# Decay rows of a Mamba-2 scan: stored head by head, and broadcast from ScalarE's DMA queue instead of GpSimd's

## The chip, the core and the metric

One core of one Trainium2 chip runs the whole kernel. The metric is the device time of one execution in microseconds (us). Before the change it is 2491.99 us, the median of three runs (2491.88, 2491.99 and 2496.45). About 0.2%, some 5 us, is the smallest change that such a measurement can tell from none.

## The reference, cut to what matters

One encoder layer on 512 tokens of width 2048: an adaLN-modulated RMSNorm, one input projection, an HGRN2 mixer (8 heads) and a Mamba-2 SSD mixer (4 groups of 4 heads), an output projection, then a gated convolutional FFN and a last norm. The change touches one factor of the SSD mixer, the decay matrix `seg`:

```python
acum = jnp.cumsum((dt * a_head).transpose(0, 1, 3, 4, 2), axis=-1)
seg = jnp.exp(jnp.where(mask, acum[..., :, None] - acum[..., None, :], -jnp.inf))
cb = jnp.einsum('bctgn,bcsgn->bcgts', cm, bm)
y_diag = jnp.einsum('bcgts,bcgrts,bcsgrp->bctgrp', cb, seg, xdt)
```

For each of the 16 heads the kernel needs acum(t) along the free axis, the same in all 128 partitions, minus acum(s) per partition.

## The kernel before, in words

All large products run on TensorE as three matmuls (L168 to L170, the product of a rounded high part and a low part). A weight chunk of 256 rows by 512 columns is loaded by SyncE into a buffer `raw` (L148), rounded by ScalarE to `whi` (L163), and VectorE takes the rest as `wlo` (L164). There are five `raw` buffers and two each of `whi` and `wlo`. The modulation vectors come from a second stream of loads: `m` from `w_mod` (L184), 512 KB each, uses the same five buffers and the same SyncE queue, and VectorE folds each into `macc` with one instruction per half (L191).

While a projection streams through, small pieces of the mixers are put between its matmuls. Here these are `ssd_mix(g)` for groups 0, 3, 2, 1, two at a time, between 287 and 456 us of the span. Its steps, in the order of the text:

- `cbm` (L425, L429): four matmuls of C and B, masked by VectorE.
- `decay(h)` for each of four heads (L433 to L443): one row of `acrow` in DRAM is broadcast to all partitions of a tile `mm` (L436), then VectorE adds the per-partition term (L439) and clamps (L441), ScalarE takes the exponential (L442), VectorE multiplies by `cbm` (L443). `mm` is one of nine buffers of 128 x 512 that all small temporaries share.
- transposes (L451, L464), states (L474 to L482), and per head the product of `mm` with `xdt` (L489), whose result VectorE adds to `y` (L494); for three heads also the contribution of the state (L499, L501, L505).

The small products use only two PSUM banks (`mis`), so a small matmul can wait until VectorE has read an earlier one; TensorE takes its instructions in order, and then the projection behind it waits too.

`acrow` is made once by `ssd_dt` (L398 to L401): 64 rows, one per quarter of the sequence and head, of 128 tokens, stored by a DMA of GpSimd's queue at 260 us.

The order on each engine is fixed when the program is built, by the tile scheduler. Every engine issues in order: a DMA issue that waits for a buffer holds back what stands behind it on that engine. DMAs of the hardware queues (SyncE's and ScalarE's) also take turns on eight completion semaphores, shown below as DMAHW0 to DMAHW7, and a DMA is issued only when the one before it on its semaphore has landed. GpSimd's DMAs have semaphores of their own (DMASW).

Of the kernel before, what the change touches and what calls it, by code (L numbers as in the profile page):

```python
# [7 lines left out]
F32 = mybir.dt.float32  # L8
# [6 lines left out]
P = 128  # L15
S = 512
# [18 lines left out]
def hybrid_block_kernel(  # L35
# [6 lines left out]
    nc = tc.nc  # L42
# [22 lines left out]
    def T(name="t", dtype=F32):  # L65
        return tmp.tile([P, 512], dtype, tag="t", name=nm(name))
# [10 lines left out]
    def MIS(name="mis"):  # L77
        return psm.tile([P, 512], F32, tag="mis", name=nm(name))
# [4 lines left out]
    def CT(shape, name, dtype=F32):  # L83
        return cst.tile(shape, dtype, tag=name, name=name)
# [3 lines left out]
    def bc(ap, shape):  # L88
        return ap.unsqueeze(len(ap.shape)).broadcast_to(shape)
# [265 lines left out]
        A.activation(out=xbc[g][:, which, :], in_=y, func=AF.Silu)  # L355

    drm = ctx.enter_context(tc.tile_pool(name="drm", bufs=1, space=bass.MemoryType.DRAM))
    acrow = drm.tile([64, P], F32, tag="acrow", name="acrow")
    dtt = CT([P, 64], "dtt")
    dta = CT([P, 64], "dta")  # L360
    negb = CT([P, 16, 4, 2], "negb")
# [2 lines left out]
    def ssd_dt(src):  # L364
        pt = MIS()
        for t in range(NT):
            PE.transpose(out=pt[:, t * P:(t + 1) * P], in_=src[:, t * P:(t + 1) * P], identity=ident)
        xb, e, z, z2, p = (T(s_)[:, 0:64] for s_ in ("xb", "en", "zz", "z2", "pp"))

        def c4(t_):  # L370
            return t_.rearrange("p (c h) -> p c h", c=4)

        V.tensor_tensor(out=c4(xb), in0=c4(pt)[:, :, 0:16], in1=dtb.unsqueeze(1).broadcast_to([P, 4, 16]), op=ALU.add)
        V.tensor_tensor(out=c4(xb), in0=c4(pt)[:, :, 64:80], in1=c4(xb), op=ALU.add)
        V.scalar_tensor_tensor(out=e, in0=xb, scalar=-1.0, in1=xb, op0=ALU.mult, op1=ALU.min)
        A.activation(out=e, in_=e, func=AF.Exp)
        V.tensor_scalar(out=z, in0=e, scalar1=2.0, scalar2=None, op0=ALU.add)
        V.reciprocal(out=z, in_=z)
        V.tensor_tensor(out=z, in0=z, in1=e, op=ALU.mult)
        V.tensor_tensor(out=z2, in0=z, in1=z, op=ALU.mult)  # L380
        V.tensor_scalar(out=p, in0=z2, scalar1=1.0 / 19, scalar2=None, op0=ALU.mult)
        for k in (17, 15, 13, 11, 9, 7, 5, 3):
            V.scalar_tensor_tensor(out=p, in0=p, scalar=1.0 / k, in1=z2, op0=ALU.add, op1=ALU.mult)
        V.scalar_tensor_tensor(out=p, in0=p, scalar=1.0, in1=z, op0=ALU.add, op1=ALU.mult)
        V.tensor_scalar(out=xb, in0=xb, scalar1=0.0, scalar2=None, op0=ALU.max)
        V.scalar_tensor_tensor(out=dtt, in0=p, scalar=2.0, in1=xb, op0=ALU.mult, op1=ALU.add)
        V.tensor_tensor(out=c4(dta), in0=c4(dtt), in1=an.unsqueeze(1).broadcast_to([P, 4, 16]), op=ALU.mult)
        pc = MIS()
        for i, m in enumerate((tri, suf, ones, tri64, l1m)):
            PE.matmul(out=pc[:, i * 64:(i + 1) * 64], lhsT=m, rhs=dta, start=True, stop=True)  # L390
        A.activation(out=e3.rearrange("p a b -> p (a b)"), in_=pc[:, 0:192], func=AF.Exp)
        V.tensor_scalar(out=negb[:, :, :, 0].rearrange("p h c -> p c h"),
                        in0=pc[:, 192:256].rearrange("p (c h) -> p c h", h=16),
                        scalar1=-1.0, scalar2=None, op0=ALU.mult)
        V.tensor_copy(out=negb[:, :, :, 1].rearrange("p h c -> p c h"),
                      in_=pc[:, 256:320].rearrange("p (c h) -> p c h", h=16))
        pr = MIS()
        PE.matmul(out=pr[0:64, 0:P], lhsT=dta, rhs=tri64, start=True, stop=True)  # L398
        ar = T("acr")
        V.tensor_copy(out=ar[0:64, 0:P], in_=pr[0:64, 0:P])  # L400
        nc.gpsimd.dma_start(out=acrow, in_=ar[0:64, 0:P])  # L401

    def ssd_mix(g):

# [28 lines left out]
        def decay(h):  # L433
            hh = 4 * g + h
            m = mt[h] = T("mm")
            nc.gpsimd.dma_start(out=m.rearrange("p (c t) -> p c t", c=4),  # L436
                                in_=acrow.rearrange("(c h) t -> h c t", h=16)[hh].partition_broadcast(P))
            m8 = m.rearrange("p (a t) -> p a t", a=8)
            V.tensor_tensor(out=m8, in0=m8, in1=bc(negb[:, hh, :, :].rearrange("p c b -> p (c b)"), [P, 8, 64]),  # L439
                            op=ALU.add)  # L440
            V.tensor_scalar(out=m, in0=m, scalar1=0.0, scalar2=None, op0=ALU.min)  # L441
            A.activation(out=m, in_=m, func=AF.Exp)  # L442
            V.tensor_tensor(out=m, in0=m, in1=cbm, op=ALU.mult)  # L443

        decay(0)
        for cp in range(2):
            ps = MIS()
            for cc in range(2):
                for b in range(2):
                    t = 2 * cp + cc  # L450
# [33 lines left out]
        for h in range(4):  # L484
            if h < 3:
                decay(h + 1)
            ps = MIS()
            for cch in range(4):
                PE.matmul(out=ps[:, cch * HD:(cch + 1) * HD], lhsT=mt[h][:, cch * P:(cch + 1) * P],  # L489
                          rhs=xdt[:, cch, h * HD:(h + 1) * HD], start=True, stop=True)  # L490
                yield 0
            for cp in range(2):
                yh = ycols(cp)[:, :, h * HD:(h + 1) * HD]
                V.tensor_tensor(out=yh, in0=yh, in1=ps[:, cp * 128:(cp + 1) * 128].rearrange("p (t f) -> p t f", t=2),  # L494
                                op=ALU.add)
            if h < 3:
                ps = MIS()
                cch = h + 1
                PE.matmul(out=ps[:, 0:256], lhsT=xb[:, 3, cch * P:(cch + 1) * P], rhs=hst[h], start=True, stop=True)  # L499
                t = T("yo")[:, 0:256]  # L500
                V.tensor_tensor(out=t.rearrange("p (h f) -> p h f", h=4),  # L501
                                in0=ps[:, 0:256].rearrange("p (h f) -> p h f", h=4),
                                in1=bc(eac[:, cch, hs], [P, 4, HD]), op=ALU.mult)
                yo = yv(cch)[:, g * 256:(g + 1) * 256]
                V.tensor_tensor(out=yo, in0=yo, in1=t, op=ALU.add)  # L505
                yield 0
# [255 lines left out]
    for st, k0, k1 in SEGMENTS:  # L762
# [44 lines left out]
        if k1 == KT and st == 2:  # L807
            ssd_dt(dtraw)
# [54 lines left out]
    for j in range(2):  # L863
# [5 lines left out]
        for t in range(NT):  # L869
            sg = T("gs")  # L870
            A.activation(out=sg, in_=accs[t], func=AF.Silu)
            for i in range(4):
                h = 4 * j + i
# [208 lines left out]
```

## Time and profile before

| What | Value |
|---|---|
| median of three runs | 2491.99 us |
| profiled execution, own time | 2497.32 us |
| its span, first to last instruction | 2495.6 us |
| TensorE busy | 2416.4 us, 97% |
| VectorE busy | 1490.2 us, 60% |
| ScalarE busy | 783.7 us, 31% |
| GpSimd busy | 55.7 us, 2% |
| data moved by DMA | 335.86 MB, mean 135 GB/s |
| the 16 broadcasts `mm<-acrow` | 256 KB each, 9.2 us from issue to landing (median) |

Times in the profile are microseconds from the start of the span. A wait is named by the engine and line that waited, an arrow, and the line that ended it. "acc" tiles are projection accumulators, "mis" tiles the small PSUM banks. The column PEclk is the clock that TensorE was granted, 1.00 being the full one.

### The profile page before, as it was taken

How to read it: one execution, taken by the hardware profiler on the slowest of the kernel's cores; microseconds unless marked ns; L12 is line 12 of the kernel's file. 1: busy time of each engine (PE TensorE's matmuls, PEld its weight loads, DVE VectorE, ACT ScalarE, POOL GpSimd, SP SyncE). 2: the span in 40 equal slices, each digit the busy share in tenths (PEclk: the TensorE clock that was granted, in tenths of full speed). 3: DMA queues.
4: the chain of work that ended last, by engine and by line, in shares of the span. 5: the costliest groups of instructions: out<-in, count | busy, mean ns of one | idle time of the engine just before them, and what ended most of it. 6: DMA issues, size and time to landing. Idle time of an engine off the chain costs nothing.

```text
span 2495.6 us, 28998 instructions
## 1 busy us (share of the span) xinstructions
PE 2416.4 (97%) x11071; PEld 1987.7 (80%) x11071; DVE 1490.2 (60%) x2262; ACT 783.7 (31%) x1135; POOL 55.7 (2%) x80
## 2 busy tenths in 40 slices
PE   6999998999999999999999999999999999999998
PEld 5777877788777777887888888888888888888887
DVE  6884866666776656668536363636354545454557
ACT  6323422333332322433232222222222222222323
POOL 4000000000000000000000000000000000000000
PEclk9999999999999999999999999999999999999999
DMA  9883575344555656366333323233333333332332
GB/s 289 257 273 105 116 128 107 90 118 135 168 161 187 243 189 199 121 220 219 93 101 93 101 93 100 94 98 96 96 99 95 100 94 101 93 101 93 102 127 85
DMA packets 262823, 335.86 MB, mean 135 GB/s; under 512 B 18092, under 2 KB 182524, under 8 KB 261404
## 3 DMA queue, kind: packets, MB, share of 16 engines
q1 hardware_dynamic: 260432, 327.42, 41.8%
q0 software_dynamic: 1568, 4.31, 2.3%
q10 hardware_dynamic: 684, 2.28, 0.3%
q8 instruction: 87, 1.43, 0.2%
q14 instruction: 52, 0.43, 0.1%
HBM read 329.72 MB, written 4.23 MB: 134 GB/s over the span
## 4 chain that ended last, share of the span: by engine, by line
PE 76%; DMA 11%; DVE 9%; issue 2%; ACT 2%; POOL 0%; SPq 0%; DVEq 0%; ACTq 0%; POOLq 0%
PE acc L170 24%; PE acc L168 24%; PE acc L169 24%; DMA m<-in_w_mod_dram 8%; DVE wlo L164 3%; DVE macc L191 2%; DMA raw<-in_w_in_dram 1%; DVE macc L240 1%; DMA x<-in_x_dram 1%; ACT whi L163 1%; PE mis L570 1%; POOL rstd L267 0%; DMA mm<-acrow 0%; PE mis L612 0%; DVE att L577 0%
## 5 line engine op out<-in xcount | busy, mean ns | idle before, releaser
L164 DVE TENSOR_TENSOR wlo<-raw,whi 128x1024 fp32r<-128x1024 f32 (+1 forms) x408 | 490.3, 1203 | 707.7 <-ACT whi L163 703.2
L163 ACT CAST whi<-raw 128x1024 fp32r<-128x1024 f32 (+2 forms) x416 | 424.6, 1022 | 1304.4 <-PE acc L169 512.2
L168 PE MATMUL acc<-hhi,whi 128*128 128x512 f32 x1920 | 770.1, 402 | 10.7 <-ACT whi L163 6.1
L170 PE MATMUL acc<-hhi,wlo 128*128 128x512 f32 x1920 | 750.1, 393 | 3.1 <-DVE wlo L164 3.1
L169 PE MATMUL acc<-hlo,whi 128*128 128x512 f32 x1920 | 751.7, 392 | 0.0
L168 PEld LDWEIGHTS acc<-hhi,whi 128*128 128x128 f32 x1920 | 362.2, 189 | 88.2 <-ACT whi L163 10.2
L170 PEld LDWEIGHTS acc<-hhi,wlo 128*128 128x128 f32 x1920 | 362.3, 189 | 83.0 <-DVE wlo L164 6.1
L169 PEld LDWEIGHTS acc<-hlo,whi 128*128 128x128 f32 x1920 | 362.8, 189 | 69.5 <-issue 1.2
L191 DVE SCALAR_TENSOR_TENSOR macc<-m,cT,macc 128x512 f32<-128x512 f32 x240 | 180.0, 750 | 127.9 <-DMA m<-in_w_mod_dram 124.5
L168 PE MATMUL acc<-whi,act 128*128 128x512 f32 x640 | 249.0, 389 | 0.0
L169 PE MATMUL acc<-wlo,act 128*128 128x512 f32 x640 | 249.0, 389 | 0.0
L170 PE MATMUL acc<-whi,act 128*128 128x512 f32 x640 | 249.0, 389 | 0.0
L168 PE MATMUL acc<-whi,hhi 128*128 128x512 f32 x384 | 163.2, 425 | 0.0
L170 PE MATMUL acc<-whi,hlo 128*128 128x512 f32 x384 | 153.7, 401 | 0.0
L169 PE MATMUL acc<-wlo,hhi 128*128 128x512 f32 x384 | 152.8, 398 | 0.0
L170 PEld LDWEIGHTS acc<-whi,act 128*128 128x128 f32 x640 | 120.1, 188 | 25.0
L168 PEld LDWEIGHTS acc<-whi,act 128*128 128x128 f32 x640 | 120.1, 188 | 24.9
L169 PEld LDWEIGHTS acc<-wlo,act 128*128 128x128 f32 x640 | 120.1, 188 | 24.9
L994 DVE TENSOR_TENSOR g<-acc,gate 128x512 f32<-128x512 f32 x160 | 105.4, 685 | 3.8
L995 DVE TENSOR_TENSOR x<-x,g 128x512 f32<-128x512 f32 x160 | 105.3, 684 | 0.0
L168 PE MATMUL acc<-mhi,whi 128*128 128x512 f32 x256 | 105.2, 411 | 0.0
L170 PE MATMUL acc<-mhi,wlo 128*128 128x512 f32 x256 | 101.1, 395 | 2.3 <-DVE wlo L164 2.3
(274 smaller groups left out, 2193.9 us busy)
## 6 DMA issues: line engine op xcount, KB each, us to landing
raw<-in_ffn_w_up_dram SPq DMA_DIRECT2D x352, 256.0 KB, 2.9
m<-in_w_mod_dram SPq DMA_DIRECT2D x128, 512.0 KB, 4.1
raw<-in_ffn_w_down_dram SPq DMA_DIRECT2D x88, 512.0 KB, 3.6
m<-in_w_mod_dram SPq DMA_DIRECT2D x128, 256.0 KB, 4.2
raw<-in_w_in_dram SPq DMA_DIRECT2D x96, 256.0 KB, 3.9
raw<-in_w_in_dram SPq DMA_DIRECT2D x48, 512.0 KB, 4.0
raw<-in_w_out_dram SPq DMA_DIRECT2D x32, 512.0 KB, 4.5
x<-in_x_dram SPq DMA_DIRECT2D x8, 1024.0 KB, 10.8
```

The lines of the kernel that those rows point to most:

```text
L163: A.copy(out=h_, in_=r_)
L164: V.tensor_tensor(out=l_, in0=r_, in1=h_.bitcast(F32), op=ALU.subtract)
L168: PE.matmul(out=ps, lhsT=lh, rhs=rh, start=first, stop=False)
L169: PE.matmul(out=ps, lhsT=lh, rhs=rl, start=False, stop=False)
L170: PE.matmul(out=ps, lhsT=ll, rhs=rh, start=False, stop=last)
L191: V.scalar_tensor_tensor(out=acc, in0=last[:, k, :], scalar=cT[:, kt:kt + 1], in1=acc, op0=ALU.mult, op1=ALU.add)
L240: V.scalar_tensor_tensor(out=acc, in0=m[:, k, :], scalar=cT[:, kt:kt + 1], in1=acc, op0=ALU.mult, op1=ALU.add)
L570: PE.matmul(out=o, lhsT=kk[:, pr * P:(pr + 1) * P], rhs=halves(q, lv, True, base=pr * P, pairs=1), start=True, stop=True)
L994: V.tensor_tensor(out=m, in0=accs[t], in1=gates[5][:, cs], op=ALU.mult)
L995: V.tensor_tensor(out=x1[t][:, cs], in0=x1[t][:, cs], in1=m, op=ALU.add)
```

## The change

`acrow` is laid out with one row of 512 tokens per head instead of 64 rows of 128. The store (L401) scatters its 64 rows accordingly and stays on GpSimd's queue. Each broadcast (L436) then reads one contiguous row of 2 KB per partition instead of four pieces of 512 B, and it is issued by ScalarE on its hardware queue instead of by GpSimd on the software queue. From L437 on, the lines of the changed file are one lower than before.

```diff
-    acrow = drm.tile([64, P], F32, tag="acrow", name="acrow")
+    acrow = drm.tile([16, S], F32, tag="acrow", name="acrow")
...
-        nc.gpsimd.dma_start(out=acrow, in_=ar[0:64, 0:P])
+        nc.gpsimd.dma_start(out=acrow.rearrange("h (c t) -> c h t", c=4), in_=ar[0:64, 0:P])
...
             m = mt[h] = T("mm")
-            nc.gpsimd.dma_start(out=m.rearrange("p (c t) -> p c t", c=4),
-                                in_=acrow.rearrange("(c h) t -> h c t", h=16)[hh].partition_broadcast(P))
+            nc.scalar.dma_start(out=m, in_=acrow[hh].partition_broadcast(P))
```

The 16 broadcasts leave GpSimd's stream, where nothing stood between them, and now stand among ScalarE's roundings and exponentials. SyncE's order is the same as before; TensorE's and VectorE's differ in places by one to four instructions between 310 and 456 us of the old span.

The first place is ScalarE around 307 us: the convolution of the last group (`cy`, `xbc`), roundings (`whi`), and the first exponentials of `mm`. Before:

```order
L351 ACTIVATE cy_2446<-xbc_128,p_679 128x512
L163 CAST whi_2649<-raw_2648 128x1024
L355 ACTIVATE xbc_128<-cy_2446 128x512
L442 ACT_TABLE_LOAD
L442 ACTIVATE mm_2511<-mm_2511 128x512
L442 ACTIVATE mm_2524<-mm_2524 128x512
```

After:

```order
L351 ACTIVATE cy_2446<-xbc_128,p_679 128x512
L436 DMA mm_2511<-acrow 128x512
L436 DMA mm_2524<-acrow 128x512
L436 DMA mm_2710<-acrow 128x512
L163 CAST whi_2649<-raw_2648 128x1024
L436 DMA mm_2723<-acrow 128x512
L355 ACTIVATE xbc_128<-cy_2446 128x512
L441 ACT_TABLE_LOAD
L441 ACTIVATE mm_2511<-mm_2511 128x512
L441 ACTIVATE mm_2524<-mm_2524 128x512
```

The first four broadcasts, which GpSimd issued from 286.70 us on, now come behind the last convolution step of ScalarE.

The second place is ScalarE around 376 us, where the second pair of groups begins; these rows are of the changed program, with the semaphores that each waits for:

```order
L163 CAST whi_3090<-raw_3089 128x1024 [waits DMAHW0_49,DMAHW1_49,DVE_49,PE_49]
L436 DMA mm_3048<-acrow 128x512 [waits DMAHW5_49]
L436 DMA mm_3061<-acrow 128x512 [waits DMAHW7_49]
L436 DMA mm_3259<-acrow 128x512 [waits DMAHW1_49]
L436 DMA mm_3272<-acrow 128x512 [waits DMAHW3_49]
L441 ACTIVATE mm_3048<-mm_3048 128x512 [waits DVE_49]
L441 ACTIVATE mm_3061<-mm_3061 128x512 [waits DVE_49]
L163 CAST whi_3137<-raw_3136 128x1024 [waits DMAHW2_49,PE_49,Activation_49]
```

In the program before, the rounding `whi_3137` stood ahead of the exponential of `mm_3061`, and the four broadcasts were issued by GpSimd between 356 and 362 us. The wait on DMAHW3 at the last of them is for the load `m_3236` of the modulation stream, that on DMAHW1 for a piece of `raw_3229`.

The third place is ScalarE around 434 us, at the last two heads of the second pair. Before:

```order
L163 CAST whi_3509<-raw_3508 128x1024
L442 ACTIVATE mm_3438<-mm_3438 128x512
L163 CAST whi_3554<-raw_3553 128x1024
L442 ACTIVATE mm_3449<-mm_3449 128x512
```

After:

```order
L163 CAST whi_3509<-raw_3508 128x1024 [waits PE_49,Activation_49]
L436 DMA mm_3438<-acrow 128x512 [waits DMAHW5_49]
L436 DMA mm_3449<-acrow 128x512 [waits DMAHW7_49,DVE_49]
L441 ACTIVATE mm_3438<-mm_3438 128x512 [waits DVE_49]
L163 CAST whi_3554<-raw_3553 128x1024 [waits DMAHW2_49,DMAHW3_49,PE_49,Activation_49]
L441 ACTIVATE mm_3449<-mm_3449 128x512 [waits DVE_49]
```

The broadcast of `mm_3438`, issued at 425.01 us by GpSimd before, now follows the rounding `whi_3509`; that of `mm_3449` waits for VectorE's L505, as it did before.

## The prediction

> **What bounds the kernel now.** I read the page first, then the waits of TensorE in the stretch of the broadcasts, then what VectorE waited for there, and then the DMA queues. The page, with span, busy time, queues and the start of the chain that ended last:
>
> ```profile
> span 2495.6 us, 28998 instructions
> PE 2416.4 (97%) x11071; PEld 1987.7 (80%) x11071; DVE 1490.2 (60%) x2262; ACT 783.7 (31%) x1135; POOL 55.7 (2%) x80
> ...
> q1 hardware_dynamic: 260432, 327.42, 41.8%
> q0 software_dynamic: 1568, 4.31, 2.3%
> q10 hardware_dynamic: 684, 2.28, 0.3%
> ...
> PE 76%; DMA 11%; DVE 9%; issue 2%; ACT 2%; POOL 0%; SPq 0%; DVEq 0%; ACTq 0%; POOLq 0%
> ```
>
> TensorE is the bound: 97% busy, so the whole kernel has 79 us in which it stands. A change to 16 small transfers can only win where TensorE stands, or loses where it now does not. The broadcasts run from 286 to 456 us. That stretch as one row (length, then busy time per engine with counts, granted TensorE clock, DMA share, GB/s), and TensorE's waits in it (total, times, longest):
>
> ```profile
> 286.00:456.00 170.00, 155.63 (x759) 127.44 (x757) 120.01 (x220) 52.04 (x70) 12.02 (x16) 0.97 0.64 118
> ...
> PE mis L499 <- DVE y L494: 7.9, 2, 4.2
> PE mis L499 <- DVE yo L501: 4.2, 1, 4.2
> PE mis L451 <- DVE cbm L429: 2.0, 2, 1.8
> ```
>
> TensorE stands 170 - 155.63 = 14.4 us here, and the three rows name 7.9 + 4.2 + 2.0 = 14.1 of it: four stops of 3.7, 1.8 (with 0.2 behind it), 4.2 and 4.2 us. Each is a small product that waits until VectorE has read a PSUM bank. There is a second loss: the clock is 0.97 over the stretch, that is 0.03 x 170 = 5.1 us of work, and it lies right behind three of the stops:
>
> ```profile
> 345.00:350.00 5.00, 1.88 (x6) 1.62 (x7) 5.00 (x12) 1.15 (x2) 0.00 (x0) 0.88 0.91 66
> 350.00:355.00 5.00, 5.00 (x22) 4.14 (x22) 1.64 (x5) 1.05 (x1) 0.00 (x0) 0.78 0.59 188
> 430.00:435.00 5.00, 3.93 (x12) 3.18 (x12) 3.37 (x10) 2.10 (x3) 0.00 (x0) 0.66 0.84 144
> 445.00:450.00 5.00, 3.23 (x11) 2.67 (x12) 4.84 (x11) 1.91 (x2) 0.00 (x0) 0.78 0.01 3
> 450.00:455.00 5.00, 5.00 (x27) 4.33 (x26) 0.99 (x3) 0.01 (x1) 0.00 (x0) 0.88 0.75 210
> ```
>
> Shortfalls of 0.12, 0.22, 0.34, 0.22 and 0.12 times 5 us give 5.1 again. Why was VectorE late? Its waits in the stretch, and the four pieces of the chain (start, length) that lie ahead of the stops:
>
> ```profile
> DVE macc L191 <- DMA m<-in_w_mod_dram: 18.1, 4, 6.2
> DVE mm L439 <- DMA mm<-acrow: 4.7, 1, 4.7
> ...
> 334.65 8.36 DMA m<-in_w_mod_dram
> ...
> 370.65 6.10 DMA m<-in_w_mod_dram
> ...
> 416.65 9.10 DMA m<-in_w_mod_dram
> ...
> 436.99 8.15 DMA mm<-acrow
> ```
>
> VectorE works in order; three times it stood at L191 for an `m` load that took 6.1 to 9.1 us, the fourth time at L439 for a broadcast of 8.15 us. The `m` loads are slow because of the broadcasts. Here is GpSimd's queue from 334 to 346 us (packets, MB, share of the 16 DMA engines), the landing time of the broadcasts, and that of SyncE's `raw` (L148) and `m` (L184) loads between 372 and 402 us, where no broadcast runs:
>
> ```profile
> q0 software_dynamic: 189, 0.64, 75.5%
> ...
> DMA to landing us min/median/max: 8.2/9.2/12.0
> ...
> DMA to landing us min/median/max: 3.0/3.5/4.2
> ...
> DMA to landing us min/median/max: 3.7/4.2/4.7
> ```
>
> With the broadcasts gone an `m` lands in 4.2 us. So all four stops hang on these 16 transfers: 0.64 MB held three quarters of the DMA engines for 12 us.
>
> **What the change does to that.** *Removed: DMA time.* The software queue's 2.3% of 2495.6 us is 57.4 us of all 16 engines, for 4.31 MB, nearly all of it broadcasts. The nearest row for the new form is q10, ScalarE's own queue: 0.3% is 7.5 us for 2.28 MB, nearly all of it two broadcasts of a DRAM row to 128 partitions. At that price 4.2 MB cost 14 us instead of about 56, or 0.9 us per broadcast instead of 3.5. Landing, one row of each kind (a broadcast of 1 MB from ScalarE's queue; the cost of its issue in ns):
>
> ```profile
> gate<-in_b_mod_dram ACTq DMA_DIRECT2D x1, 1024.0 KB, 4.9
> ...
> L259 ACTq DMA_DIRECT2D gate<-in_b_mod_dram x1: 396/396/396, 1039.3 to 1039.3; - x1
> ```
>
> A broadcast of a quarter of that size, and of the size of a `raw` piece, should land in between 3.0 (the quickest piece) and 4.9 us; I take 3.5, the median piece. Then `m_3035`, issued at 334.65, lands near 339 instead of 343.0, even with two broadcasts (1.8 us of the engines) beside it; `m_3236` near 375 instead of 376.8; `m_3605` near 421 instead of 425.8. VectorE is 4, 2 and 4 to 5 us earlier, about the length of the stops they cause (3.7, 2.0, 4.2). The fourth stop is the broadcast `mm_3449` itself: 3.9 us from issue to landing instead of 8.2, against 4.2. So the gain is at most 14.4 + 5.1 = 19.5 us, at least nothing.
>
> *Added: 16 issues on ScalarE.* 16 x 0.4 = 6.3 us on an engine that is busy 52 of 170 us here; its own time is cover enough. What counts is the place of each issue in ScalarE's order, for what it waits for holds back the next rounding `whi`, and `whi` feeds TensorE. The rows of ScalarE and VectorE at the three places of the order shown above:
>
> ```profile
> 306.98 0.82 ACT L351 ACTIVATE cy<-xbc,p 128x512 f32<-128x512 f32 x1
> ...
> 315.84 1.03 ACT L163 CAST whi<-raw 128x1024 fp32r<-128x1024 f32 x1
> ...
> 375.16 1.05 ACT L163 CAST whi<-raw 128x1024 fp32r<-128x1024 f32 x1 [5.79 <-PE acc L169]
> ...
> 384.31 1.05 ACT L163 CAST whi<-raw 128x1024 fp32r<-128x1024 f32 x1 [1.94 <-PE acc L169]
> ...
> 434.05 1.05 ACT L163 CAST whi<-raw 128x1024 fp32r<-128x1024 f32 x1 [2.67 <-issue]
> ...
> 309.98 0.69 DVE L439 TENSOR_TENSOR mm<-mm,negb 128x512 f32<-128x512 f32 x1
> 310.86 1.23 DVE L164 TENSOR_TENSOR wlo<-raw,whi 128x1024 fp32r<-128x1024 f32 x1 [0.19 <-ACT whi L163]
> ...
> 380.56 0.68 DVE L439 TENSOR_TENSOR mm<-mm,negb 128x512 f32<-128x512 f32 x1
> ```
>
> First place: `mm_2511` can be issued only at 306.98 + 0.82 = 307.8, and VectorE wants it at 309.98. Landing at 310.8 to 312.7, it holds VectorE 0.8 to 2.7 us. Behind it stands `wlo_2650`, which ended at 312.1; TensorE wants it when the chunk before is done, which the rounding at 315.84 marks, so 3.7 us of cover. But the transposed products behind it (L457 to L460) hand back PSUM banks with no visible slack, so part may reach TensorE: 0 to 2.7, I take 1.5 us. This cost is gone if the broadcast lands within 2.2 us.
>
> Second place: the issue of `mm_3272` waits for `m_3236`, 370.65 + 4.2 = 374.9, while the rounding ahead ends at 376.2. No wait; `mm_3048` lands at 376.2 + 0.4 + 3.5 = 380.1, VectorE wanted it at 380.56, and the next rounding stood at 384.31: nothing, with 3 us of cover for the two exponentials now ahead of it. SyncE waits for broadcasts too, on the shared semaphores, but for ones issued a chunk or more earlier.
>
> Third place: `mm_3438` is issued after 435.1 instead of 425.0 and lands at 439.0, two microseconds after VectorE is ready; half of that is caught by the slack that the fourth stop had: 0 to 2, I take 1 us. ScalarE's next rounding comes only 6 us after this one, so no `whi` is late.
>
> The store of `acrow` at 260 us has 47 us until its first reader: nothing.
>
> The sum: 14.4 + 5.1 - 1.5 - 1 = 17.0, less 0.5 for small waits that remain, so 16.5 us off the profiled execution's own 2497.3 us: 2480.8. That execution is 5.3 us above the median, one of the three timed runs is nearly as long (2496.45) and two are at 2491.9. One stop with the low clock behind it is worth 4.2 + 1.7 = 5.9 us, so I read the two times as the same program with one stop more or less, and such a difference goes with the stops. If it lies elsewhere, the median becomes 2475.5. I say 2480.
>
> **A rule that speaks against it.** The rows above put the cost on the queue and the form of the broadcast. The Trainium skill (DMA: Bandwidth & Descriptors, section Issuing engines are not separate DMA queues) says that DMAs issued by ScalarE, SyncE or GpSimd run on the same 16 engines and interleave, and that another issuer saves only the issue time. By that rule the `m` loads would stay as late as they are. The trace speaks against it as far as it goes: 13 us per MB on q0, 3.3 on q10.
>
> **The rivals.** *A, the queue is not the cost.* The same 4.2 MB interleave with the same loads, so the three stops behind `m` stay, and only the fourth shrinks: 2492 to 2496, no change. For it: all queues share the DMA engines. Against it: the q0 and q10 rows. 0.08.
>
> *B, slower: the broadcast is slow in any queue.* If 128 readers of one short row cost what they cost now, landing stays at 9.2 us, but issue is later. Then `mm_2511` lands at 317.0, 7 us after VectorE wants it (3.3 beyond the cover), `mm_3048` at 385.8, 5.2 late, `mm_3438` at 444.7, 7.7 late: 16 us on top of what is there, 2497 + 16 = 2513. It decides from a landing of some 6 us on. For it: no row shows a 2 KB row broadcast from ScalarE's queue. Against: 1 MB landed in 4.9 us. 0.07.
>
> *C, half.* ScalarE stands at the issues (for a buffer, or for a load on its semaphore), VectorE and `whi` are held once per pair of heads, and half of 19.5 us comes back: 2487.5, between 2484 and 2491. For it: eight of the issues wait for loads of SyncE's stream. Against: those loads are older than the buffers. 0.13.
>
> The forecast, all four stops gone or nearly: 0.72, between 2474 and 2486.
>
> **How the numbers follow.** 0.2% is 5 us: faster is below 2487. Faster: 0.72, and 0.08 of C, 0.80. Same: 0.05 of C and A's 0.08, 0.13. Slower: B, 0.07. The range reaches down to 2471 (19.5 off the median of 2492 would be 2472.5) and up to 2491, C's end; it leaves out B and most of A.
>
> **What would show it.** Right: the landing of `mm<-acrow` at 3 to 5 us, the `m` loads from 330 to 430 us near 4.2 us, no TensorE wait at L499 or L451 over 1 us, the clock of that stretch at 0.99 or more, and VectorE's L439 waiting 1 to 3 us once or twice for its DMA. Wrong: L439 waits of 4 us or more, `whi` roundings that come later behind the issues, or `m` loads still at 6 to 9 us; or gaps closed here that open again past 500 us.

## The result, and the profile after

The changed kernel takes 2478.78 us, the median of four runs (2477.34 to 2479.94), against 2494.22 us for the kernel before in runs beside it on the same chip: a ratio of 0.9937, with a 95% interval of 0.9924 to 0.9949. The forecast was 2480, faster. The profiled execution took 2477.3 us, 20.0 less than the profiled one of before. One of the four runs of a later kernel, the one with pieces 1 KB apart, took 2547.1 us at a granted clock of 0.96 and is left out of that kernel's median and ratio.

The page of the changed kernel, with its span, the busy times and the two queues that carry (q10) or carried (q0) the broadcasts (packets, MB, share of 16 engines):

```profile
span 2475.6 us, 28950 instructions
...
PE 2408.1 (97%) x11071; PEld 1980.7 (80%) x11071; DVE 1490.1 (60%) x2262; ACT 784.7 (32%) x1135; POOL 43.8 (2%) x64
...
q10 hardware_dynamic: 2988, 6.47, 0.8%
...
q0 software_dynamic: 304, 0.12, 0.0%
```

The stretch of the broadcasts as one row, and three slices of 5 us out of it (length, then busy time of TensorE, its weight loads, VectorE, ScalarE and GpSimd with counts, granted clock, DMA share, GB/s):

```profile
286.00:456.00 170.00, 166.80 (x835) 137.15 (x834) 128.29 (x234) 59.00 (x84) 0.00 (x0) 1.00 0.42 124
...
310.00:315.00 5.00, 4.06 (x18) 3.01 (x17) 3.62 (x6) 2.57 (x4) 0.00 (x0) 1.00 0.45 137
...
380.00:385.00 5.00, 3.63 (x18) 2.74 (x17) 4.76 (x8) 0.53 (x1) 0.00 (x0) 1.00 0.34 87
...
445.00:450.00 5.00, 5.00 (x29) 4.26 (x28) 2.00 (x3) 1.81 (x3) 0.00 (x0) 1.00 0.00 0
```

TensorE now stands 170 - 166.80 = 3.2 us where it stood 14.4, and the clock is 1.00 where it was 0.97, in the slice from 445 us for example, which had 3.23 us of work at a clock of 0.78 before. Idle time and low clock together are what the stretch loses: 14.4 + 5.1 = 19.5 us before, 3.2 now, so 16.3 of the 20.0 us were found here. What is left of the stops, from TensorE's waits between 250 and 480 us (total, times, longest), and the two stops themselves in its instructions in order of time (start, length, and in brackets the idle time and what ended it):

```profile
PE mis L450 <- DVE y L457: 2.9, 2, 1.5
...
PE mis L498 <- DVE y L493: 0.2, 1, 0.2
```

```profile
315.55 0.63 PE L450 MATMUL mis<-ident,xbc 128*128 128x128 f32 x4 [1.49 <-DVE y L457]
...
384.02 0.41 PE L450 MATMUL mis<-ident,xbc 128*128 128x128 f32 x2 [1.37 <-DVE y L457]
```

The four stops of before (at L499 twice, L499 behind L501, L451) are gone. Two of some 1.4 us are new, both at the transposes (L450 is L451 of before), which wait until VectorE's L457 has read a PSUM bank. VectorE is late there because of its own waits, in the same window:

```profile
DVE macc L191 <- DMA m<-in_w_mod_dram: 7.0, 4, 3.8
DVE mm L438 <- DMA mm<-acrow: 5.8, 7, 1.7
```

The 18.1 us at L191 have become 7.0; the waits for broadcasts are seven small ones where there was one of 4.7. The landing of the broadcasts, and that of the `m` loads between 330 and 430 us:

```profile
DMA to landing us min/median/max: 3.1/4.7/7.3
...
DMA to landing us min/median/max: 3.7/4.4/5.1
```

The landing, the `m` loads and the clock are what the prediction named as signs of being right. Two of its signs fail: it allowed no stop over 1 us at L499 or L451, and there are two of 1.4 and 1.5 at L450; and it had VectorE waiting for broadcasts once or twice, where it waits seven times. Of the rest of the 20.0 us, 2.2 lie in the 544 us behind the stretch (528.4 us of TensorE's work now, 526.3 before, in the same length); the gain isn't given back.

### The profile page after: what moved, and what is told of

Read it like the earlier page. It is cut to its first block, busy times and chain, and to the rows that moved or that the text cites. A ratio compares the mean times of both kernels' runs of the same rounds, so it can differ in the third digit from the quotient of the medians.

```text
span 2475.6 us, 28950 instructions
## 1 busy us (share of the span) xinstructions
PE 2408.1 (97%) x11071; PEld 1980.7 (80%) x11071; DVE 1490.1 (60%) x2262; ACT 784.7 (32%) x1135; POOL 43.8 (2%) x64
## 4 chain that ended last, share of the span: by engine, by line
PE 75%; DMA 10%; DVE 10%; ACT 2%; issue 2%; POOL 0%; SPq 0%; ACTq 0%; DVEq 0%; POOLq 0%
PE acc L170 24%; PE acc L168 24%; PE acc L169 24%; DMA m<-in_w_mod_dram 8%; DVE wlo L164 3%; DVE macc L191 2%; DVE macc L240 1%; DMA raw<-in_w_in_dram 1%; ACT whi L163 1%; PE mis L569 1%; DMA mm<-acrow 0%; PE mis L488 0%; DMA x<-in_x_dram 0%; POOL rstd L267 0%; DVE att L576 0%
## 5 line engine op out<-in xcount | busy, mean ns | idle before, releaser
L168 PEld LDWEIGHTS acc<-hhi,whi 128*128 128x128 f32 x1920 | 361.3, 188 | 89.5 <-ACT whi L163 12.2
L191 DVE SCALAR_TENSOR_TENSOR macc<-m,cT,macc 128x512 f32<-128x512 f32 x240 | 180.1, 750 | 115.3 <-DMA m<-in_w_mod_dram 111.7
```

The source lines that it names most:

```text
L168: PE.matmul(out=ps, lhsT=lh, rhs=rh, start=first, stop=False)
L191: V.scalar_tensor_tensor(out=acc, in0=last[:, k, :], scalar=cT[:, kt:kt + 1], in1=acc, op0=ALU.mult, op1=ALU.add)
```

## The experiments

The theory of the prediction: the software queue made the broadcasts, and through them the `m` loads, slow. Its rivals: the layout did it, or neither. The time of each run stands beside runs of the kernel before on the same chip (2496.3 us for the first four kernels, 2491.1 for the next four, 2496.8 for three and 2496.4 for the last).

### The queue alone

```diff
-            nc.gpsimd.dma_start(out=m.rearrange("p (c t) -> p c t", c=4),
+            nc.scalar.dma_start(out=m.rearrange("p (c t) -> p c t", c=4),
                                 in_=acrow.rearrange("(c h) t -> h c t", h=16)[hh].partition_broadcast(P))
```

> One part of the change alone: the broadcasts go to ScalarE's hardware queue, but acrow keeps 64 rows of 128, so each partition still takes four pieces of 512 B. Theory Q (the software queue is what made the transfers slow): as fast as the whole change, 2476 to 2482 us; landing of mm<-acrow 4 to 6 us, their share of the DMA engines under 20 us in all instead of 56, no TensorE stop over 2 us between 286 and 440 us. Rival L (the 512 B pieces made them slow): the broadcasts stay at 3 us or more of the engines each, landing 7 us or more, and, since they are issued later than before, 2494 us or above.

Measured: 2515.1 us, ratio 1.0077 (1.0059 to 1.0094), so slower. The queue on the page, then the landing of the broadcasts and of the `m` loads from 330 to 430 us:

```profile
q10 hardware_dynamic: 9132, 6.47, 1.1%
...
DMA to landing us min/median/max: 8.2/9.5/14.9
...
DMA to landing us min/median/max: 3.8/7.0/10.2
```

TensorE's and VectorE's waits between 250 and 480 us, and the stretch as one row:

```profile
PE mis L451 <- DVE y L458: 14.3, 2, 9.0
PE mis L499 <- DVE y L494: 10.6, 3, 5.2
...
DVE mm L439 <- DMA mm<-acrow: 26.3, 8, 5.5
DVE macc L191 <- DMA m<-in_w_mod_dram: 17.2, 4, 7.4
...
286.00:456.00 170.00, 146.42 (x691) 119.50 (x690) 109.97 (x198) 46.69 (x62) 0.00 (x0) 0.92 0.39 107
```

On ScalarE's queue the same broadcasts land in 9.5 us, as on GpSimd's (9.2), and the `m` loads stay slow. Since the broadcasts are issued later (from 305.6 us on instead of 286.7), VectorE now waits 26.3 us for them. The stretch loses 23.6 us of standing and 0.08 x 170 = 13.6 of clock, 37.2 in all. The theory of the queue falls with this run.

### The layout alone

```diff
-    acrow = drm.tile([64, P], F32, tag="acrow", name="acrow")
+    acrow = drm.tile([16, S], F32, tag="acrow", name="acrow")
...
-            nc.gpsimd.dma_start(out=m.rearrange("p (c t) -> p c t", c=4),
-                                in_=acrow.rearrange("(c h) t -> h c t", h=16)[hh].partition_broadcast(P))
+            nc.gpsimd.dma_start(out=m, in_=acrow[hh].partition_broadcast(P))
```

> The other part alone: one row of 512 tokens per head, one piece of 2 KB per partition, still issued by GpSimd on the software queue. Theory Q: no change, 2490 to 2498 us, q0 still about 55 us of all 16 engines and landing near 9 us, the stops of TensorE at L499 and L451 of before still there (12 us or more in all). Rival L: as fast as the whole change, 2476 to 2482 us.

Measured: 2475.0 us, ratio 0.9913 (0.9899 to 0.9928). The software queue on the page, the issues of the broadcasts (ns of one, first and last issue) with their landing, VectorE's wait for `m` between 250 and 480 us, and the stretch:

```profile
q0 software_dynamic: 1584, 4.31, 0.6%
...
L436 POOL DMA_DIRECT2D mm<-acrow x16: 546/546/898, 286.5 to 422.8; - x16
DMA to landing us min/median/max: 3.3/3.7/4.7
...
DVE macc L191 <- DMA m<-in_w_mod_dram: 5.9, 4, 3.7
...
286.00:456.00 170.00, 169.92 (x855) 140.59 (x854) 131.32 (x241) 59.39 (x86) 9.12 (x16) 1.00 0.43 126
```

The same queue that took 57.4 us of all engines now takes 0.6% of 2476.1 = 14.9, and the broadcasts land in 3.7 us. VectorE's wait for `m` falls from 18.1 to 5.9 us, and TensorE stands 0.1 us in the stretch. The order of instructions on TensorE, VectorE, ScalarE and SyncE is that of before, so the reordering of the changed kernel isn't the cause of its gain either.

### No broadcast at all

The 16 broadcasts are left out, and L439 reads a constant tile in their place; with that the decay rows are missing from the computation.

```diff
+    zrow = CT([P, 64], "zrow")
+    V.memset(zrow, -1.0)
...
-            nc.gpsimd.dma_start(out=m.rearrange("p (c t) -> p c t", c=4),
-                                in_=acrow.rearrange("(c h) t -> h c t", h=16)[hh].partition_broadcast(P))
...
-            V.tensor_tensor(out=m8, in0=m8, in1=bc(negb[:, hh, :, :].rearrange("p c b -> p (c b)"), [P, 8, 64]),
+            V.tensor_tensor(out=m8, in0=zrow.unsqueeze(1).broadcast_to([P, 8, 64]), in1=bc(negb[:, hh, :, :].rearrange("p c b -> p (c b)"), [P, 8, 64]),
```

> Before, without the 16 broadcasts: VectorE's L439 reads a constant tile instead, so the decay rows are left out of what is computed and no small transfer runs. It shows all that the broadcasts cost in any form. If the m loads were late only because of the broadcasts: m lands in 3.7 to 5 us throughout, no stop of TensorE over 1 us between 286 and 440 us, and a time 2 to 4 us under the changed kernel's (which has two stops of 1.5 us left), 2474 to 2478 us. If the m loads are late for another reason (the five shared buffers, VectorE's load): stops stay and 2485 us or more.

Measured: 2477.8 us, ratio 0.9923 (0.9910 to 0.9936). The stretch, and VectorE's wait for `m` between 250 and 480 us:

```profile
286.00:456.00 170.00, 169.65 (x856) 140.38 (x854) 130.46 (x240) 62.13 (x88) 0.00 (x0) 1.00 0.34 101
...
DVE macc L191 <- DMA m<-in_w_mod_dram: 4.4, 2, 3.8
```

This is the floor: 0.4 us lost. The layout alone reaches it (the 2.8 us between the two medians are no difference: their intervals overlap), so nothing clear of the noise was left that another queue could gain. (Without broadcasts the order on TensorE and VectorE differs in places from that of before; in the kernel with the layout alone it does not.)

### The first row of each group from SyncE

An attempt to do away with the new stops: in the changed kernel the row of the first head of each group is issued by SyncE, the other three by ScalarE.

```diff
-            nc.scalar.dma_start(out=m, in_=acrow[hh].partition_broadcast(P))
+            q = nc.scalar if h else nc.sync
+            q.dma_start(out=m, in_=acrow[hh].partition_broadcast(P))
```

> The changed kernel with the first row of each group issued by SyncE, where its place in the order is earlier than ScalarE's; the other 12 stay on ScalarE. The two stops that the changed kernel has (2.9 us in all, at the transposes L450, which wait for VectorE's L457 behind a late mm row) should go: 2474 to 2478 us, VectorE's waits at L438 for mm<-acrow down from 5.8 us to under 3. Rival: the issue on SyncE waits for a buffer and holds the weight loads behind it, a rounding comes late, 2480 us or more.

Measured: 2486.4 us, ratio 0.9963 (0.9948 to 0.9977), 0.26% above the ratio of the changed kernel, whose interval it touches: a miss. SyncE's issues, and TensorE's and VectorE's waits:

```profile
L437 SPq DMA_DIRECT2D mm<-acrow x4: 339/422/863, 305.6 to 373.3; - x4
...
PE mis L451 <- DVE y L458: 4.7, 2, 3.8
...
DVE mm L439 <- DMA mm<-acrow: 7.9, 5, 4.9
```

SyncE issued the first row at 305.6 us, hardly earlier than ScalarE (306.6). GpSimd had done it at 286.5. In the second pair of groups SyncE's turn came at 372.2 us, and VectorE stood 4.9 us for a row there: the longer of the two stops at L451, 3.8 us, lies behind that.

### The distance between the pieces

The new layout makes one piece of four and also changes the distance between the pieces. In the layout of before, a head's four rows of 512 B lie 16 x 512 B = 8 KB apart. Three kernels on GpSimd's queue keep more than one piece: `acrow` as [4, 18, 128], that is before with two unused rows per quarter (four pieces 9 KB apart); as [16, 4, 256], of which half is read (four pieces 1 KB apart); and as [2, 16, 256] (two pieces of 1 KB, 16 KB apart). The edit of the first, which leaves the order of instructions on every engine as it was:

```diff
-    acrow = drm.tile([64, P], F32, tag="acrow", name="acrow")
+    acrow = drm.tile([4, 18, P], F32, tag="acrow", name="acrow")
...
-        nc.gpsimd.dma_start(out=acrow, in_=ar[0:64, 0:P])
+        nc.gpsimd.dma_start(out=acrow[:, 0:16, :], in_=ar[0:64, 0:P])
...
-                                in_=acrow.rearrange("(c h) t -> h c t", h=16)[hh].partition_broadcast(P))
+                                in_=acrow.rearrange("c h t -> h c t")[hh].partition_broadcast(P))
```

> Before, with two unused rows per quarter of acrow, so that a head's four pieces of 512 B lie 9 KB apart instead of 8 KB; GpSimd's queue, and nothing else changed. Theory P (number of pieces): as before, 2490 to 2500 us, landing 8 to 12 us. Theory D in the form that a distance of just 8 KB makes the pieces collide: landing 3 to 5 us, 2472 to 2480 us.

> The layout alone on GpSimd's queue, but with acrow padded so that a head's four pieces of 512 B lie 1 KB apart (in before they lie 8 KB apart, in the layout-alone kernel they touch and form one piece of 2 KB). The order on all other engines is that of the layout-alone kernel. Theory P (the number of pieces, 512 reads of 512 B instead of 128 of 2 KB, is the cost): landing 8 to 12 us and a time as before, 2490 to 2500 us. Theory D (the distance of 8 KB between the pieces is the cost): landing 3 to 5 us, 2472 to 2479 us.

> Between the two layouts: two pieces of 1 KB per partition, 16 KB apart, stored by two DMAs; GpSimd's queue. Theory P: the price lies between, some 1.7 us of all 16 engines per broadcast (3.5 in before, 0.9 with one piece of 2 KB), landing 5 to 7 us, 2478 to 2490 us. Theory D: with two places far apart still colliding, landing 5 us or more and 2480 to 2495 us; if it lands in under 4 us neither holds as put.

Measured: 9 KB apart 2473.4 us, ratio 0.9923 (0.9905 to 0.9941); 1 KB apart 2472.7, ratio 0.9926 (0.9906 to 0.9945); two pieces 2474.6, ratio 0.9929 (0.9910 to 0.9949). Of the first, the software queue, the landing and the stretch:

```profile
q0 software_dynamic: 1584, 4.31, 0.6%
...
DMA to landing us min/median/max: 3.6/4.3/5.7
...
286.00:456.00 170.00, 169.23 (x849) 139.82 (x848) 131.35 (x239) 59.80 (x86) 12.95 (x16) 1.00 0.42 125
```

Of the two pieces 16 KB apart, the queue and the landing:

```profile
q0 software_dynamic: 1632, 4.31, 1.3%
...
DMA to landing us min/median/max: 4.9/5.8/6.7
```

One KB of padding per quarter does all that the change did, with queue, order, number and size of pieces as before. So the cost was the 8 KB between the pieces of a row. Two pieces 16 KB apart stand between: 1.3% of 2473.5 us is 32 us, 2.0 per broadcast. Their time came out below both ranges expected for it (from 2478 and from 2480 us on): a landing of 5.8 us, issued this early, kept VectorE waiting for broadcasts for 1.8 us only, and the stretch lost 3.3 us.

### The changed kernel beside these

The unchanged text of the changed kernel, run with these three.

> The changed kernel again, beside the others on one chip, to compare it with the layout alone through the ratio to before. All theories: ratio 0.992 to 0.995, two stops of some 1.5 us at the transposes L450 behind late mm rows.

Measured: 2476.8 us, ratio 0.9937 (0.9922 to 0.9952), 3.4 us above the padded kernel; the intervals overlap, so the times alone don't tell the two apart. Its stretch lost 3.7 us of standing and, at a clock of 0.99, 1.7 more; that of the padded kernel 0.8.

### The padded layout on ScalarE's queue

The kernel of the queue alone, with the padding of 1 KB per quarter added.

```diff
-    acrow = drm.tile([64, P], F32, tag="acrow", name="acrow")
+    acrow = drm.tile([4, 18, P], F32, tag="acrow", name="acrow")
...
-        nc.gpsimd.dma_start(out=acrow, in_=ar[0:64, 0:P])
+        nc.gpsimd.dma_start(out=acrow[:, 0:16, :], in_=ar[0:64, 0:P])
...
-            nc.gpsimd.dma_start(out=m.rearrange("p (c t) -> p c t", c=4),
-                                in_=acrow.rearrange("(c h) t -> h c t", h=16)[hh].partition_broadcast(P))
+            nc.scalar.dma_start(out=m.rearrange("p (c t) -> p c t", c=4),
+                                in_=acrow.rearrange("c h t -> h c t")[hh].partition_broadcast(P))
```

> The broadcasts keep their four pieces of 512 B, 9 KB apart as in the padded kernel, and are issued by ScalarE's queue as in the kernel with the queue alone. Theory P (the 8 KB distance is the cost, the queue is not): landing falls from 9.5 us (queue alone) to 4.3 to 5.5, VectorE's wait for broadcasts from 24 us to some 5 to 8, and the time from 2515 to 2476 to 2481, as the changed kernel or a little above the padded one. Rival (ScalarE's queue needs the one contiguous row to be quick): landing 7 us or more and 2495 to 2513.

Measured: 2481.0 us, ratio 0.9938 (0.9924 to 0.9951). Queue, landing, TensorE's waits and the stretch:

```profile
q10 hardware_dynamic: 9132, 6.47, 0.9%
...
DMA to landing us min/median/max: 3.1/4.9/8.3
...
PE mis L451 <- DVE y L458: 4.6, 2, 2.6
PE mis L499 <- DVE y L494: 1.3, 1, 1.3
...
286.00:456.00 170.00, 164.07 (x814) 134.87 (x813) 124.64 (x228) 56.85 (x81) 0.00 (x0) 0.99 0.42 124
```

On ScalarE's queue, too, the padding takes the landing from 9.5 to 4.9 us and the time from 2515.1 to 2481.0. Four pieces or one row makes little difference there. The stops at L451 that the changed kernel has are here as well, while GpSimd's kernels with a quick layout have none. So they go with the issue on ScalarE, where the first one is at 305.5 to 306.6 us instead of 286.5, and VectorE waits for the landing (7.5 us here, 5.8 in the changed kernel, 1.0 in the padded one). The order on TensorE and VectorE, which that issue changes too, is the same in this kernel, in the changed one and with the queue alone; it was not tested apart from the issue.

### Which distances are slow

Three more on GpSimd's queue, with 32 or 24 rows per quarter (pieces 16 or 12 KB apart), and with [2, 4, 8, 128] (4 KB apart). The edit of the second, whose store and read are those of the kernel with 9 KB:

```diff
-    acrow = drm.tile([64, P], F32, tag="acrow", name="acrow")
+    acrow = drm.tile([4, 24, P], F32, tag="acrow", name="acrow")
```

> As before, GpSimd's queue, only that a head's four pieces lie 16 KB apart instead of 8. Theory P1 (a distance that is a multiple of 8 KB puts the four pieces in each other's way): landing 8 to 10 us, 3 us or more of all engines per broadcast, 2487 to 2496. Rival P2 (8 KB alone is bad, or what matters is the place of the 32 KB block): landing 4 to 6 us, 2472 to 2479.

> As before, GpSimd's queue, only that a head's four pieces lie 4 KB apart instead of 8 (two blocks of eight heads; the store is four DMAs). If all large powers of two are slow: landing 8 to 10 us and 2487 to 2496. If only distances from 8 KB on are: landing 4 to 6 us, about 1 us of all engines per broadcast, 2472 to 2479. If it is a matter of degree: some 6 us and 2 us per broadcast, and 2474 to 2480, since the other kernel with 2 us per broadcast lost nothing by it.

> As before, GpSimd's queue, only that a head's four pieces lie 12 KB apart instead of 8. Of the layouts measured so far the price follows how many of the four pieces have the same place modulo 8 KB: one (contiguous, 1 KB and 9 KB apart) 0.9 us of all engines per broadcast and landing 3.7 to 4.3; two (4 KB apart, two pieces 16 KB apart) 1.9 to 2.0 and 5.3 to 5.8; four (8 and 16 KB apart) 3.4 to 3.6 and 8.9 to 9.2. At 12 KB the pieces stand at 0, 4, 0 and 4 KB modulo 8. Theory M (this count sets the price): some 1.9 us, landing 5.3 to 5.8, like 4 KB apart, and 2474 to 2484. Rival (only distances that are powers of two are slow): 0.9 us, landing 4.3. Rival (it gets slower with the distance from 9 KB to 16 KB, or multiples of 4 KB are all slow): 3.4 us, landing 9.

Measured: 16 KB 2494.0 us, ratio 0.9990 (0.9981 to 0.9999); 4 KB 2482.9, ratio 0.9942 (0.9930 to 0.9955); 12 KB 2482.9, ratio 0.9934 (0.9909 to 0.9959). The time at 4 KB lies 2.9 us above the range expected for a matter of degree; price and landing (1.9 and 5.3 us) are near what was expected there (2 and 6). The queue and the landing of the pieces 16 KB apart:

```profile
q0 software_dynamic: 1584, 4.31, 2.2%
...
DMA to landing us min/median/max: 7.8/8.9/11.9
```

And of those 12 KB apart:

```profile
q0 software_dynamic: 1584, 4.31, 1.2%
...
DMA to landing us min/median/max: 4.9/5.4/6.7
```

All layouts on GpSimd's queue, ordered by how many pieces of a row have the same place modulo 8 KB (their distances from the row's first piece leave the same remainder by 8 KB). The price is the queue's share of the span over 16 broadcasts; the page gives that share to 0.1%, which is 0.15 us per broadcast, and shows 0.1% on this queue without any broadcast:

| Pieces of a row | same place mod 8 KB | all 16 engines, per broadcast | landing, median |
|---|---|---|---|
| 1 of 2 KB | 1 | 0.9 us | 3.7 us |
| 4, 1 KB apart | 1 | 0.9 us | 4.2 us |
| 4, 9 KB apart | 1 | 0.9 us | 4.3 us |
| 4, 4 KB apart | 2 | 1.9 us | 5.3 us |
| 4, 12 KB apart | 2 | 1.9 us | 5.4 us |
| 2 of 1 KB, 16 KB apart | 2 | 2.0 us | 5.8 us |
| 4, 16 KB apart | 4 | 3.4 us | 8.9 us |
| 4, 8 KB apart (before) | 4 | 3.6 us | 9.2 us |

The first kernels gave the count, and the 12 KB run was forecast by it. It fell where it should, neither with the slow ones nor with the quick ones, though 12 KB is no power of two. That the count sets the price is a rule that fits eight layouts; what it is in the memory that pieces with the same place share was not seen.

One more table, which closes the account: what the stretch lost in each profile (standing plus low clock), what that says against the 19.5 us of before, and the measured difference of the medians.

| Kernel | lost in the stretch | so, against before | measured |
|---|---|---|---|
| changed | 3.2 + 0 | -16.3 | -15.4 |
| queue alone | 23.6 + 13.6 | +17.7 | +18.8 |
| layout alone | 0.1 + 0 | -19.4 | -21.3 |
| no broadcast | 0.4 + 0 | -19.1 | -18.5 |
| first rows from SyncE | 5.6 + 1.7 | -12.2 | -9.9 |
| 9 KB apart | 0.8 + 0 | -18.7 | -17.7 |
| 1 KB apart | 1.4 + 0 | -18.1 | -18.4 |
| two pieces 16 KB apart | 3.3 + 0 | -16.2 | -16.5 |
| changed, again | 3.7 + 1.7 | -14.1 | -14.3 |
| 16 KB apart | 13.6 + 3.4 | -2.5 | -2.8 |
| 4 KB apart | 3.6 + 0 | -15.9 | -13.9 |
| 12 KB apart | 3.3 + 0 | -16.2 | -13.5 |
| 9 KB apart, ScalarE's queue | 5.9 + 1.7 | -11.9 | -15.8 |

All agree within 4 us, although one profiled execution stands against medians and the clock is read to 0.01, which is 1.7 us here. To that accuracy the stretch from 286 to 456 us is the whole effect, in both directions.

## Why the prediction was right, and where it was wrong

**What bounds, and what there was to gain: right.** The four stops and the low clock behind three of them were worth 19.5 us by the prediction; without any broadcast 19.1 of these are gone, and 18.5 us of time. That the stops came from slow `m` loads and one slow broadcast, and that the 16 broadcasts made the `m` loads slow, holds too: without broadcasts the wait at L191 falls from 18.1 to 4.4 us.

**Why the broadcasts were slow: wrong.** The step that failed is the sentence that "the rows above put the cost on the queue and the form of the broadcast", with "13 us per MB on q0, 3.3 on q10" behind it. The two rows differed in two things: the queue, and what was read (pieces 8 KB apart there, long rows here). The prediction let the price stand for the queue and for the form together. Taken apart, the queue's share is nothing or a loss (2515.1 us with the queue alone), and the form is all of it (2475.0 with the layout alone). Within the form it isn't the short pieces or their number either, but their distance: 2473.4 with four pieces 9 KB apart. The time came out right because the change also contained the layout; as far as the queue is concerned, that was luck.

**The rule of the Trainium skill that was set aside: right.** The prediction held the q0 and q10 rows against the statement of the Trainium skill (DMA: Bandwidth & Descriptors, section Issuing engines are not separate DMA queues) that another issuer saves only its issue time. The runs agree with the rule: with the same 8 KB pieces a broadcast landed in 9.2 us from one queue and 9.5 from the other, with 9 KB in 4.3 and 4.9. The rule speaks of the issuer alone, and the layout changed in the same edit. The Trainium skill (DMA: Bandwidth & Descriptors, section Latency and other measured facts) also has an entry by which copies with 4 or 8 MiB between the rows of neighbouring partitions ran at 103 GB/s and, with 4 KiB of padding on the 4 MiB, at 214. The runs here show the like for pieces 8 and 16 KB apart, and 1 KB of padding on the 8 KB mends it.

**"0.64 MB held three quarters of the DMA engines": true of the software queue, but not the reason.** In the queue-alone kernel an `m` load took 10.2 us from 341 us on, while the engines were 29.2% busy with broadcasts and 15.5% with SyncE's loads (341 to 352 us). So a share of three quarters is not needed to make `m` late. What the `m` loads waited for instead stays open: these shares are means over 16 engines and do not show whether single ones were full. The prediction's reading came from a share that the software queue counts otherwise (below).

**Rival B: its mechanism was real, and the layout kept it away.** "The broadcast is slow in any queue" was worked out at 2513 us, with a landing of 9.2 us and later issue. The queue alone gave 9.5 us and 2515.1. What spoke against it in the prediction, 1 MB landed in 4.9 us, was a broadcast of another pattern. Rival A said that the queue is not the cost, which is so; its time (2492 to 2496) took the layout for nothing. Rival C, half of the gain through ScalarE's order, did not come: 3.2 us were left, not ten.

**The terms of the sum.** Price: 0.9 us per broadcast was taken; q10 gives (0.8% of 2475.6, less the 7.5 us that the other rows of that queue took) / 16 = 0.8. Landing: 3.5 taken, range 3.0 to 4.9; measured 4.7, up to 7.3. The `m` loads: 4.2 taken, 4.4 measured.

First place: 0 to 2.7, taken 1.5, measured 1.49. ScalarE's issues there and at the second place, with the convolution step ahead of the first, and VectorE's waits, from their instructions in order of time:

```profile
306.57 0.82 ACT L351 ACTIVATE cy<-xbc,p 128x512 f32<-128x512 f32 x1
306.58 1.31 ACTq L436 DMA_DIRECT2D mm<-acrow  x3
...
371.55 1.77 ACTq L436 DMA_DIRECT2D mm<-acrow  x4
...
311.38 0.69 DVE L438 TENSOR_TENSOR mm<-mm,negb 128x512 f32<-128x512 f32 x1 [1.73 <-DMA mm<-acrow]
...
380.24 0.69 DVE L438 TENSOR_TENSOR mm<-mm,negb 128x512 f32<-128x512 f32 x1 [0.68 <-DMA mm<-acrow]
```

The issue came 1.2 us earlier than taken, 0.8 of it since it did not wait for the end of the convolution step ahead of it (306.57 + 0.82), and the landing took 1.3 longer, 4.78 us. The two errors cancel; that the 1.5 was met is luck.

Second place: taken as nothing, measured 1.37. This is the term that was mis-sized. The prediction followed the first broadcast of the group only (it lands in time), but four are issued within 1.8 us, and the last landed 7.3 us after its issue:

```profile
372.88 7.33 DMA mm<-acrow
```

VectorE stood there three times (0.5, 0.9 and 0.7 us), and the transposes behind it were late. Third place: 0 to 2, taken 1; nothing was left there but the 0.2 us at L498. Small waits: 0.5 taken. In sum 3.0 us were taken off the gain for the new form and 3.2 measured, with the second and the third place exchanged: the sum held by luck. The 16.5 us could be taken off two times of before, the profiled execution's 2497.3 or the median's 2492.0, and the forecast went by the first. The stretch of the profiled executions gave 16.3; the medians, 2494.2 before with a fourth run, differ by 15.4.

**The better version.** On GpSimd's queue both the new layout (2475.0 us) and the padding (2473.4) lose next to nothing in the stretch, where the changed kernel loses 3.2 to 5.4 us. Beside the same runs of before the padded kernel is ahead of the changed one by 0.14% (0.9923 against 0.9937), less than the intervals tell apart, so the queue's 3 us are shown by the traces and not by the times.

## What to carry to other kernels

When two rows of a trace have a different price, list everything that differs between them before the price is given to one of it; and where an edit changes two things, work out the time of each alone, since here one was worth -21 us and the other +19 alone. Where all partitions read the same few pieces of DRAM, look at the distance between the pieces, and try a little padding before another queue. An issuer with nothing else to do (GpSimd here, 20 us ahead of ScalarE) hides a landing for which VectorE has to wait when the issue stands later, among ScalarE's other work.

## What the runs showed of the hardware that was not expected

- A broadcast of a row in pieces to 128 partitions cost about 0.9, 1.9 or 3.5 us of all engines, by the software queue's share, as one, two or four of its pieces had the same place modulo 8 KB. The cause inside the memory is open.
- Such broadcasts slowed other loads while the DMA engines were less than half busy in the mean: 10.2 us for an `m` load at 45% (341 to 352 us of the queue-alone kernel), where 4.2 us was the median without broadcasts beside it (372 to 402 us before).
- The busy share of a queue is not one measure for both kinds. With the same pieces 8 KB apart, landing in 9.2 and 9.5 us, the software queue showed 57 us, and ScalarE's queue 1.1% of 2511.5, less 7.5, which is 20. With 9 KB it was 15 on either. So here the landing times were compared across queues, and the shares were not.
- GpSimd's queue was the quicker one where the layout was good: 3.7 us of landing against 4.7 for the same rows from ScalarE's, which were issued in groups of up to four; the queue and the grouping were not told apart.
